# Feed-forward of a hybrid trunk step: borders of the up product rearranged

## The chip, the cores and the metric

The program runs on one core of one Trainium2 chip. The metric is the device time of one execution in microseconds; the median of the runs shown counts. One execution was also taken by the hardware profiler, and all rows below come from it.

## The reference

One layer of a bidirectional hybrid (RWKV-7 and mLSTM) diffusion step on 128 context and 1024 latent tokens, D_MODEL 1024, D_FF 2816, all in float32. The change lies in the last third: the output projection with its norm, and the gated ConvFFN.

```python
x = x + g1 * rmsnorm(merged @ p['w_out'], p['norm_g'][1])
h = rmsnorm(x, p['norm_g'][2]) * (1.0 + sc2) + sh2
u_act, u_val = jnp.split(h @ p['ffn_up'], 2, axis=-1)
u_act = dwconv_grid(u_act, p['ffn_conv'], rows) + p['ffn_conv_b']
f = (jax.nn.silu(u_act) * u_val) @ p['ffn_down']
x = x + g2 * rmsnorm(f, p['norm_g'][3])
```

`dwconv_grid` is a 3x3 depthwise convolution on a grid 64 wide (of width 3 on the context). There are 128 + 1024 = 1152 tokens, T in the kernel.

## The kernel before, in words

Every float32 product is made of reduced-precision parts: an operand is split into a high part (written by ACT, `AF.Copy`) and a low part (DVE, the difference), and TensorE (PE) makes three products of parts. So each weight tile and each activation needs one ACT and one DVE instruction before PE can use it. A scheduler orders the instructions of each engine; where an engine's `.on` is true, its instructions stay in the order in which the code is written. PE is pinned in this way around here, the others are not.

**The output projection** (tile `pwo`, L1500) goes by blocks of 128 tokens, nine of them (NB). Per block: a Square with row sums on ACT (L1516), the gate rows on DVE (`ob`, L1517), the residual (`xt`, L1521), a second Square (L1524), the second norm (`ob`, L1526), and `modulate`: eight transposes on PE (`ptx`), scale and shift on DVE and ACT into `hf` (L1482, L1485), and a store of `hf` to `h2d` in HBM by the DMA queue of SP. The last block's `modulate` is written inside the up product, ahead of unit 4. The gate rows of the second gate are stored (`grd`) at the end of this stage.

**The up product** computes two halves of 22 blocks of 128 columns (`uraw` the convolved half, `uval` the other) by a scheme of seven products P1 to P7 instead of eight. A unit is one product of one block for one half of the tokens (c 0 or 1): 12 matmuls 128x288 into `pu`. The operands of P1, P2 and P3 are quarters X11, X21, X22 of h, those of the others sums of them (T1 to T4), made and split by `x_split` and `x_rest` (L1455, L1456, sums at L1464). Half c=0 is loaded into `x0` and `x1` during the output projection; half c=1 is loaded into the `xb` tiles by `x_mid` and `x_late`, which are written ahead of units 4 and 8. Units 0 to 3 are P1 and P2 of blocks 0 and 1 for c=0, units 4 to 7 the same for c=1, unit 8 is the first P6. The weights come as `wraw`; P6 needs a sum `s` of two quarters, made by POOL (L1625) into the one buffer with tag `hf`, and differences (L1626 on POOL, L1627, L1628 on DVE). `w_split` writes `hl`, high on ACT (L1632), low on DVE (L1633). Products leave `pu` on DVE (L1671 to L1682), P1 on ACT (L1669).

**The convolution** of a finished block (`conv_of`): one bias and scale on ACT (L1637), eight taps and two context operations on DVE (L47, L50), Silu on ACT (L1641), the product with `uval` on POOL (L1642), and a store to `f2d` (L1643). It runs beside the units of the next block. For the blocks in LATE it is put off: `uraw` and `uval` are stored to `latd`, and the convolution is made during the down product by `late_convs`, with tiles `lraw`, `lval` (two buffers) and `lua` (one).

**The down product** has three sweeps over the tokens, of 4, 3 and 2 blocks of 128. The first reads each of the 22 blocks of f once, in the order KO, in which the LATE blocks are the last. `f_group` fetches f in groups of six blocks, by pairs, into `fg` (each pair: a DMA, a split on ACT L1708 and DVE L1709); the buffers of groups 0, 1 and 2 are those of `x1`, `x0` and `x2`. The products go into `pfd`; the weights are split at L1718 and L1719.

```python
PROD = ("P1", "P2", "P6", "P7", "P4", "P5", "P3")
LATE = (1, 5, 9, 13, 17, 21)
KO = [i for i in range(NFB) if i not in LATE] + list(LATE)
s1s[i] = wt.tile([128, 4, 128], F32, name="s1", tag="hf", bufs=1)
if (m, c) == ("P3", 1):
    conving = (put_off if i in LATE else conv)(i)
```

Of the kernel before, what the change touches and what calls it, by code (L numbers as in the profile page):

```python
# [58 lines left out]
def _body(tc, ctx, A, O, dbg, stop):  # L59
# [88 lines left out]
    latd = dram("latd", [6, 2, 128, T])  # L148
# [1238 lines left out]
    with tc.tile_pool(name="br", bufs=1) as bp, tc.tile_pool(name="brl", bufs=2) as bl:  # L1387
# [11 lines left out]
        banks(pg=5, ps=3)  # L1399
# [66 lines left out]

    def modulate(xh, b):

        c = 0 if b == 0 else 1
        for q in range(2):  # L1470
            pt = (pss if b < NB - 1 else psg)([128, 4, 128], "ptx")
            for j in range(4):
                f = 4 * q + j
                pe.transpose(pt[:, j, :], xh[:, 128 * f:128 * f + 128], ident)
            if q == 0 or b == NB - 1:
                hf = wt.tile([128, 4, 128], F32, name="hf", tag="hf", bufs=1)
            else:
                hf = wp.tile([128, 8, 128], F32, name="hf", tag="whi", bufs=2)[:, 0:4]
            for j in range(4):
                f = 4 * q + j  # L1480
                if j % 2:
                    s.activation(hf[:, j, :], pt[:, j, :], AF.Identity, scale=sc2[:, f, c:c + 1],  # L1482
                                 bias=sh2[:, f, c:c + 1])
                else:
                    v.tensor_scalar(hf[:, j, :], pt[:, j, :], sc2[:, f, c:c + 1], sh2[:, f, c:c + 1],  # L1485
                                    op0=ALU.mult, op1=ALU.add)
            dma(h2d[q][:, :, 128 * b:128 * b + 128], hf)

    with tc.tile_pool(name="wo", bufs=1) as wop:
# [15 lines left out]
        for blocks in ((0, 1),) + tuple((b,) for b in range(2, NB)):  # L1505
            pts = {b: [psg([128, 512], "pwo") for q in range(2)] for b in blocks}
            wo_mm(pts, blocks)
            for b in blocks:
                c = 0 if b == 0 else 1
# [35 lines left out]
        rows_out(1, make_scale("g2", 40, 3, 0.0))  # L1545
# [24 lines left out]
    def x_mid():  # L1570

        x_load(1, 0, 0, q11)
        x_load(1, 1, 0, q21)
        x_split(1, "X11", q11, xb[1], xb[2])
        x_split(1, "X21", q21, xb[3], xb[8])
        x_rest(0, ta, tb, (r11, r12, r21, r22), [quarter(x2, i) for i in range(4)])

    def x_late():
        x_load(1, 0, 1, q12)
        x_load(1, 1, 1, q22)  # L1580
        x_split(1, "X22", q22, xb[9], xb[10])
        ta = x_sub(v, x_tmp(), q12, q11)
        tb = x_sub(v, x_tmp(), q22, ta)
        x_rest(1, ta, tb, (q11, q12, q21, q22), [xb[0]] + xb[11:14])

    PROD = ("P1", "P2", "P6", "P7", "P4", "P5", "P3")
# [7 lines left out]
    LATE = (1, 5, 9, 13, 17, 21)  # L1594
# [25 lines left out]
    def w_split(i, m):  # L1620

        a11, a12, a21, a22 = raws[i]
        if m == "P6":
            s1s[i] = wt.tile([128, 4, 128], F32, name="s1", tag="hf", bufs=1)
# [21 lines left out]
    with tc.tile_pool(name="cv", bufs=2) as cv:  # L1646
# [51 lines left out]
        def f_group(sw, j):  # L1698
# [6 lines left out]
            for o in range(0, n, 2):  # L1705
                hi, lo = (t_[:, x, o:o + 2, 0:128 * nb] for x in range(2))
                dma(f32(lo), f2d[6 * j + o:6 * j + o + 2, :, ts].rearrange("k p t -> p k t"))
                s.activation(hi, f32(lo), AF.Copy)  # L1708
                v.tensor_tensor(lo, f32(lo), f32(hi), op=ALU.subtract)  # L1709
                yield  # L1710
# [11 lines left out]
        pe.on = True  # L1722
        conving, ns, wds = None, 0, {}
        w_load()
        w_load()
        for u, (i, m, c) in enumerate(units):
            if u == 4:
                modulate(ob, NB - 1)
                x_mid()
# [7 lines left out]
            if u == 8:  # L1737
                x_late()
            unit(i, m, c)
            if conving:  # L1740
                next(conving, None)
            if (m, c) == ("P3", 1):
# [4 lines left out]
            if i == NFB - 1 and c == 1 and m == "P6":  # L1747
                g0 = f_group(0, 0)
                next(g0)
            if i == NFB - 1 and c == 1 and m == "P4":  # L1750
                wds[0] = wd_split(0)
        for _ in conving:
# [6 lines left out]
    with tc.tile_pool(name="fd", bufs=1) as fd, tc.tile_pool(name="fo", bufs=2) as fo:  # L1759
        gr = rows_in(1, [fd.tile([128, D], F32, name=f"grow{c}") for c in range(2)])  # L1760
# [41 lines left out]
        for sw, (b0, nb) in enumerate(SWEEPS):  # L1802
# [3 lines left out]
            for k in range(no):  # L1806
# [6 lines left out]
                if k == no - 1:  # L1813
# [7 lines left out]
                for _ in range(3 + k % 2):  # L1821
                    next(late, None)
            for _ in late:
# [48 lines left out]
```

## Time and profile before

| | us |
|---|---|
| median of 3 runs | 2272.18 (2268.37 to 2274.38) |
| the profiled execution | 2274.78 |
| its span | 2272.9 |
| PE busy | 2059.0 (91%) |
| DVE busy | 1500.1 (66%) |
| ACT busy | 875.3 (39%) |
| POOL busy | 677.5 (30%) |

Engines: PE is TensorE, DVE VectorE, ACT ScalarE, POOL GpSimd; SP issues most DMAs. Times in a trace are microseconds from the span's start. The rows of windows have the stretch, its length, then busy time (and instructions) of PE, PE's weight loads, DVE, ACT and POOL, the mean granted clock of PE as a share of full speed, the busy share of the DMA engines and GB/s. The rows of a timeline have start, duration, engine, line, operation, names (out<-in), shape, how many instructions stand together, and in brackets the engine's idle time just before and what ended it. The rows of the chain have start, duration and the work that the end of the program goes back to. The rows of waits have what waited for what: us in total, times, the longest.

### The profile page before, as it was taken

The numbers are of one execution on the slowest core, as the hardware profiler recorded it, in microseconds if no ns is written. First come the engines' busy times: TensorE is split into PE (matmuls) and PEld (weight loads), VectorE is DVE, ScalarE is ACT, GpSimd is POOL, SyncE is SP. The second block draws the span as 40 slices with busy tenths as digits, with TensorE's granted clock in tenths as the row PEclk, the third lists the DMA queues.
The fourth block names the chain that finished last, engine by engine and source line by source line (L and its number), as shares of the span: only waits on it lengthen the run. The fifth ranks groups of instructions, "written<-read, shape, count | busy, mean of one in ns | idle before, by whom it ended". The sixth has DMA issues, their size and how long they took to land.

```text
span 2272.9 us, 41306 instructions
## 1 busy us (share of the span) xinstructions
PE 2059.0 (91%) x16579; PEld 1883.0 (83%) x16579; DVE 1500.1 (66%) x2355; ACT 875.3 (39%) x1662; POOL 677.5 (30%) x784
## 2 busy tenths in 40 slices
PE   6999998988889989889989999699999999895998
PEld 4998998978878878878878877699999999674776
DVE  3766778779555556654733445799999999785432
ACT  3664646462233433346421244332223232342322
POOL 2000198888522224355312101122222221111000
PEclk8999999999989999989989999899999999997999
DMA  9144444535745655377666654322121221763543
GB/s 263 53 99 120 121 120 112 146 100 135 190 112 130 157 128 140 109 216 228 193 217 202 223 189 150 89 78 100 57 98 60 97 92 51 289 245 118 199 139 102
DMA packets 405615, 322.06 MB, mean 142 GB/s; under 512 B 92817, under 2 KB 366901, under 8 KB 405424
## 3 DMA queue, kind: packets, MB, share of 16 engines
q1 hardware_dynamic: 302848, 225.78, 33.4%
q10 hardware_dynamic: 89280, 56.32, 8.7%
q0 software_dynamic: 13296, 37.33, 5.3%
q8 instruction: 131, 2.15, 0.4%
q14 instruction: 60, 0.49, 0.1%
HBM read 229.33 MB, written 90.02 MB: 141 GB/s over the span
## 4 chain that ended last, share of the span: by engine, by line
PE 49%; DMA 15%; POOL 12%; DVE 12%; issue 5%; ACT 5%; SPq 1%; ACTq 0%; POOLq 0%; DVEq 0%
PE pu L70 18%; PE pg L399 6%; POOL Lb L546 5%; POOL tmp L544 5%; PE pfd L70 5%; PE pwo L1500 4%; PE pbr L70 4%; PE pg L70 3%; DMA wraw<-in_ffn_down 2%; DVE lua L47 2%; DMA aw<-in_ada_w 1%; DMA La<-Ad 1%; PE pY L70 1%; DVE ua L47 1%; DMA bon<-bond 1%
## 5 line engine op out<-in xcount | busy, mean ns | idle before, releaser
L399 PE MATMUL pg<-act,whi 128*128 128x384 f32 (+1 forms) x1696 | 328.5, 341 | 0.5 <-DVE act L362 0.4
L70 PE MATMUL pu<-x,hl 128*128 128x288 f32 x2024 | 296.1, 297 | 11.3 <-ACT hl L1632 9.3
L399 PEld LDWEIGHTS pg<-act,whi 128*128 128x128 f32 (+1 forms) x1696 | 296.4, 189 | 7.4 <-DVE act L362 0.8
L70 PEld LDWEIGHTS pu<-x,hl 128*128 128x128 f32 x2024 | 280.3, 191 | 12.0 <-ACT hl L1632 9.5
L70 PE MATMUL pu<-xb,hl 128*128 128x288 f32 x1672 | 247.3, 295 | 2.2 <-DVE xb L1456 1.4
L70 PEld LDWEIGHTS pu<-xb,hl 128*128 128x128 f32 x1672 | 230.6, 189 | 3.0 <-DVE xb L1456 1.9
L70 PE MATMUL pfd<-whi,fg 128*128 128x512 f32 x540 | 171.4, 399 | 14.7 <-ACT whi L1718 7.1
L399 PE MATMUL pg<-act,wlo 128*128 128x384 f32 (+1 forms) x848 | 168.7, 338 | 7.8 <-DVE wlo L386 7.8
L47 DVE SCALAR_TENSOR_TENSOR ua<-uraw,par,ua 128x945 f32<-128x945 f32 (+2 forms) x128 | 161.7, 1263 | 11.0 <-ACT ua L1637 11.0
L1632 ACT ACTIVATE hl<-wraw 128x512 fp32r<-128x512 f32 x132 | 81.1, 628 | 207.2 <-PE pu L70 158.4
L399 PEld LDWEIGHTS pg<-act,wlo 128*128 128x128 f32 (+1 forms) x848 | 147.8, 186 | 11.3 <-DVE wlo L386 8.1
L386 DVE TENSOR_TENSOR wlo<-wraw,whi 128x1024 fp32r<-128x1024 f32 (+1 forms) x64 | 80.9, 1267 | 96.4 <-ACT whi L385 96.3
L70 PEld LDWEIGHTS pfd<-whi,fg 128*128 128x128 f32 x540 | 103.0, 192 | 39.4 <-ACT whi L1718 10.1
L546 POOL TENSOR_TENSOR Lb<-Lb,tmp 96x31 f32<-96x31 f32 (+15 forms) x155 | 128.5, 829 | 12.1
L544 POOL TENSOR_TENSOR tmp<-La,Lb 96x31 f32<-96x31 f32 (+15 forms) x155 | 122.6, 791 | 29.1 <-DMA La<-Ad 17.3
L1633 DVE TENSOR_TENSOR hl<-wraw,hl 128x512 fp32r<-128x512 f32 x132 | 124.4, 943 | 2.0 <-ACT hl L1632 2.0
L70 PE MATMUL pfd<-wlo,fg 128*128 128x512 f32 x270 | 108.7, 403 | 8.4 <-DVE wlo L1719 8.1
L70 PE MATMUL pfd<-wr,fg 128*128 128x512 f32 x378 | 88.6, 395 | 26.9 <-ACT fg L1708 24.2
L1642 POOL TENSOR_TENSOR uval<-uval,ua 128x1152 f32<-128x1152 f32 x16 | 44.5, 2782 | 214.9 <-ACT ua L1641 214.9
L70 PEld LDWEIGHTS pfd<-wr,fg 128*128 128x128 f32 x378 | 71.7, 190 | 43.4 <-ACT fg L1708 24.6
L70 PE MATMUL pg<-act,whi 128*128 128x384 f32 x496 | 102.5, 357 | 0.0
L1500 PE MATMUL pwo<-whi,act 128*128 128x512 f32 x288 | 95.7, 410 | 4.0 <-ACT whi L385 4.0
(440 smaller groups left out, 4118.8 us busy)
## 6 DMA issues: line engine op xcount, KB each, us to landing
wraw<-in_ffn_down SPq DMA_DIRECT2D x52, 512.0 KB
wraw<-in_w_in ACTq DMA_DIRECT2D x44, 512.0 KB
wraw<-in_ffn_up SPq DMA_DIRECT2D x44, 512.0 KB
KRd<-KR SPq DMA_DIRECT2D x24, 384.0 KB
sgz<-zraw ACTq DMA_DIRECT2D x16, 576.0 KB
KA<-KRd SPq DMA_DIRECT2D x72, 128.0 KB
BKs<-BKd SPq DMA_DIRECT2D x36, 256.0 KB
suv<-Vd POOLq DMA_DIRECT2D x72, 128.0 KB, 4.1
```

What stands on the lines that cost most here:

```text
L47: v.scalar_tensor_tensor(o, img[:, r0 + i:r1 + i, c0 + j:c1 + j], wt, o, op0=ALU.mult, op1=ALU.add)
L70: return (lambda *a, **k: tc.keep_in_program_order(f(*a, **k))) if self.on else f
L386: v.tensor_tensor(lo, raw, hi.bitcast(F32), op=ALU.subtract)
L399: pe.matmul(out, wt(hw, k), at(ha, k), start=(i == 0), stop=(i == last))
L544: e.tensor_tensor(t3, L[:, j, i].unsqueeze(2).to_broadcast([NI, n, m]), X[:, j:j + 1, c].to_broadcast([NI, n, m]), op=ALU.mult)
L546: e.tensor_tensor(X[:, i, c], X[:, i, c], t3, op=ALU.subtract)
L1500: pe.matmul(pts[b][q], AS[g][:, ha, k, 128 * o:128 * o + 128], wo2[k][hw][:, 0, 512 * q:512 * q + 512], start=(k == 0 and i == 0), stop=(k ...
L1632: s.activation(w[:, 0], src, AF.Copy)
L1633: v.tensor_tensor(w[:, 1], src, f32(w[:, 0]), op=ALU.subtract)
L1642: gp.tensor_tensor(val, val, ua, op=ALU.mult)
```

## The change

- The product order becomes P1, P2, P6, P7, P3, P4, P5; a block's convolution follows P5.
- LATE is (2, 7, 12, 17, 21) in place of (1, 5, 9, 13, 17, 21): five convolutions are put off.
- The sum `s` of block 0 gets its own buffer (one half of a `uval` tile), and the second `hf` of the last block's `modulate` the other half.
- ACT is pinned for the last block of the output projection, and again for the last `modulate` with the splits of X11 and X21 for c=1 behind it. The loads of these quarters, and the operands T1 to T4 for c=0, are written ahead of `x_mid`.
- The first group of f is fetched as two single blocks and two pairs, from P3 of the last block on (P6 before), with a second step at its P4.
- The gate rows are written at unit 60 in the code, and read back in the first down sweep behind k = 9.
- The counts of PSUM banks `pg` and `ps` stand the other way round in one call; the late convolutions advance by 3, 3, 4 steps per k in place of 3, 4.

```diff
-        banks(pg=5, ps=3)
+        banks(ps=3, pg=5)
...
-            if q == 0 or b == NB - 1:
+            if q == 1 and b == NB - 1:
+                hf = spare[0][:, 512:1024].rearrange("p (k n) -> p k n", n=128)
+            elif q == 0:
...
             for b in blocks:
+                s.on = b == NB - 1
...
-        rows_out(1, make_scale("g2", 40, 3, 0.0))
+        s.on = False
...
     def x_mid():
 
-        x_load(1, 0, 0, q11)
-        x_load(1, 1, 0, q21)
+        s.on = True
+        modulate(ob, NB - 1)
         x_split(1, "X11", q11, xb[1], xb[2])
         x_split(1, "X21", q21, xb[3], xb[8])
-        x_rest(0, ta, tb, (r11, r12, r21, r22), [quarter(x2, i) for i in range(4)])
+        s.on = False
+
+    x_load(1, 0, 0, q11)
+    x_load(1, 1, 0, q21)
+    x_rest(0, ta, tb, (r11, r12, r21, r22), [quarter(x2, i) for i in range(4)])
...
-    PROD = ("P1", "P2", "P6", "P7", "P4", "P5", "P3")
+    PROD = ("P1", "P2", "P6", "P7", "P3", "P4", "P5")
...
-    LATE = (1, 5, 9, 13, 17, 21)
+    LATE = (2, 7, 12, 17, 21)
...
-            s1s[i] = wt.tile([128, 4, 128], F32, name="s1", tag="hf", bufs=1)
+            if i == 0:
+                s1s[i] = spare[0][:, 0:512].rearrange("p (k n) -> p k n", n=128)
+            else:
+                s1s[i] = wt.tile([128, 4, 128], F32, name="s1", tag="hf", bufs=1)
...
-            for o in range(0, n, 2):
-                hi, lo = (t_[:, x, o:o + 2, 0:128 * nb] for x in range(2))
-                dma(f32(lo), f2d[6 * j + o:6 * j + o + 2, :, ts].rearrange("k p t -> p k t"))
+            for o, e in ((0, 1), (1, 2), (2, 4), (4, 6)) if sw == j == 0 else ((o, o + 2) for o in range(0, n, 2)):
+                hi, lo = (t_[:, x, o:e, 0:128 * nb] for x in range(2))
+                dma(f32(lo), f2d[6 * j + o:6 * j + e, :, ts].rearrange("k p t -> p k t"))
...
+        spare.append(cvt("uval"))
...
             if u == 4:
-                modulate(ob, NB - 1)
                 x_mid()
...
+            if u == 60:
+                rows_out(1, make_scale("g2", 40, 3, 0.0))
...
-            if (m, c) == ("P3", 1):
+            if (m, c) == (PROD[-1], 1):
...
-            if i == NFB - 1 and c == 1 and m == "P6":
+            if i == NFB - 1 and c == 1 and m == "P3":
                 g0 = f_group(0, 0)
                 next(g0)
             if i == NFB - 1 and c == 1 and m == "P4":
                 wds[0] = wd_split(0)
+                next(g0)
...
-        gr = rows_in(1, [fd.tile([128, D], F32, name=f"grow{c}") for c in range(2)])
+        gr = [fd.tile([128, D], F32, name=f"grow{c}") for c in range(2)]
...
-                if k == no - 1:
+                if k == min(no - 1, 17):
                     next(g3)
...
-                for _ in range(3 + k % 2):
+                for _ in range(3 + (k % 3 == 2)):
                     next(late, None)
+                if sw == 0 and k == 9:
+                    rows_in(1, gr)
```

ACT at the end of the output projection, before (`ob,s2o<-xt` is the last block's second Square, `xb` the splits of the second token half, `hf` the last modulate):

```order
L1669 ACTIVATE uraw<-pu 128x288
L1455 ACTIVATE x_14544<-xs 128x1152
L1455 ACTIVATE xb_14545<-xb_14548 128x1152
L1524 ACTIVATE ob,s2o<-xt_14513 128x1024
L1669 ACTIVATE uraw<-pu 128x288
L322 ACTIVATE s2o<-s2o,eps_130 128x1
L1455 ACTIVATE xb_14547<-xb_14550 128x1152
L1482 ACTIVATE hf<-ptx,modT,sc_13527 128x128
```

and now (the half of `uval` is the second `hf`; instructions of a pinned engine carry the line of the helper, L70):

```order
L1681 ACTIVATE uraw<-pu 128x288
L70 ACTIVATE ob,s2o<-xt_14513 128x1024
L70 ACTIVATE s2o<-s2o,eps_130 128x1
L1455 ACTIVATE x_14540<-xs 128x1152
L1681 ACTIVATE uraw<-pu 128x288
L1644 ACTIVATE hl<-wraw 128x512 x2
L1455 ACTIVATE x_14540<-xs 128x1152
L70 ACTIVATE hf<-ptx,modT,sc_13527 128x128 x2
L70 ACTIVATE uval<-ptx,modT,sc_13527 128x128 x2
L70 ACTIVATE xb_14541<-xb_14544 128x1152
L70 ACTIVATE xb_14543<-xb_14546 128x1152
```

The Square moved ahead of both xb splits, and the xb splits moved behind the four writes of modulate.

SP at the same place, before (`grd` is the store of the gate rows, `h2d` that of hf, `xb` the loads of the second token half):

```order
L76 DMA wraw<-in_ffn_up 128x8x128
L76 DMA h2d<-hf 512x1x128 x2
L76 DMA grd<-g_14531 128x8x1 x2
L76 DMA xb_14548<-h2d 128x4x288
L76 DMA xb_14550<-h2d 128x4x288
L76 DMA x1d<-xt_14513 128x1024
L76 DMA h2d<-hf 512x1x128
L76 DMA xb_14549<-h2d 128x4x288
```

and now:

```order
L76 DMA wraw<-in_ffn_up 128x8x128
L76 DMA h2d<-hf 512x1x128 x2
L76 DMA grd<-g_15666 128x8x1 x2
L76 DMA xb_14544<-h2d 128x4x288
L76 DMA xb_14546<-h2d 128x4x288
L76 DMA x1d<-xt_14513 128x1024
L76 DMA h2d<-hf 512x1x128
L76 DMA h2d<-uval 512x1x128
```

The store of the gate rows stands where it stood before, between the hf stores and the xb loads; the second half of the last hf store now comes out of `uval` and stands ahead of the next xb load.

SP at the end of the up product, before (`fg` are the fetches of f, `latd` the stores of the last block put off, `grow` the loads of the gate rows):

```order
L76 DMA wraw<-in_ffn_down 128x1024 x2
L76 DMA fg<-f2d 128x2x512
L76 DMA latd<-uval 128x1152
L76 DMA fg<-f2d 128x2x512
L76 DMA latd<-uraw 128x1152
L76 DMA fg<-f2d 128x2x512 x2
L76 DMA grow_19967<-grd 128x1024
```

and now:

```order
L76 DMA wraw<-in_ffn_down 128x1024
L76 DMA fg<-f2d 128x512 x2
L76 DMA wraw<-in_ffn_down 128x1024
L76 DMA fg<-f2d 128x2x512 x4
L76 DMA latd<-uval 128x1152
L76 DMA latd<-uraw 128x1152
L76 DMA wraw<-in_ffn_down 128x1024
L76 DMA fg<-f2d 128x2x512
L76 DMA lraw<-latd 128x1152
```

The first fetches are single blocks, the stores of the last block stand behind four pairs, and the gate rows' loads have gone from here to a place behind the first late loads.

## Rows read from the trace of the kernel before

**Rows 1.** Windows: the two borders and the sweep between them.
```profile
1430.00:1470.00 40.00, 26.52 (x161) 25.59 (x162) 29.91 (x41) 15.78 (x25) 7.19 (x4) 0.80 0.25 71
1470.00:1880.00 410.00, 410.00 (x3098) 410.00 (x3098) 381.46 (x565) 122.13 (x194) 106.61 (x64) 1.00 0.25 83
1940.00:2090.00 150.00, 118.03 (x494) 93.70 (x495) 105.90 (x105) 55.23 (x57) 21.39 (x12) 0.91 0.58 215
```

**Rows 2.** Waits of PE, 1290 to 1470.
```profile
PE pu L70 <- ACT hl L1632: 9.3, 1, 9.3
PE ptx L70 <- DVE ob L1526: 6.7, 1, 6.7
...
PE pu L70 <- DVE ob L1517: 2.0, 1, 2.0
```

**Rows 3.** Timeline of PE, 1414 to 1492.
```profile
1417.10 8.16 PE L70 MATMUL pu<-x,hl 128*128 128x288 f32 x48 [2.01 <-DVE ob L1517]
1431.95 1.97 PE L70 MATMUL ptx<-ident,ob 128*128 128x128 f32 x8 [6.69 <-DVE ob L1526]
1433.57 7.33 PE L70 MATMUL pu<-xb,hl 128*128 128x288 f32 x48
1450.17 12.30 PE L70 MATMUL pu<-x,hl 128*128 128x288 f32 x72 [9.28 <-ACT hl L1632]
...
1489.09 1.72 PE L70 MATMUL pu<-x,hl 128*128 128x288 f32 x12
```

**Rows 4.** The chain that ended last, 1400 to 1475.
```profile
1417.11 10.87 DMA xb<-h2d
...
1442.48 3.06 DMA h2d<-hf
...
1445.71 1.69 POOL s L1625
...
1447.47 1.26 POOL wraw L1626
```

**Rows 5.** Timeline of ACT, 1418 to 1450.
```profile
1428.00 1.16 ACT L1455 ACTIVATE xb<-xb 128x1152 fp32r<-128x1152 f32 x1 [4.16 <-DMA xb<-h2d]
1429.07 1.04 ACT L1524 ACTIVATE ob<-xt 128x1024 f32<-128x1024 f32 x1
```

**Rows 6.** Timeline of PE, 1925 to 2085.
```profile
1930.97 1.75 PE L70 MATMUL pu<-xb,hl 128*128 128x288 f32 x12
1939.80 0.79 PE L70 MATMUL pfd<-whi,fg 128*128 128x512 f32 x1 [7.08 <-ACT fg L1708]
...
2079.87 0.79 PE L70 MATMUL pfd<-wr,fg 128*128 128x512 f32 x1 [24.20 <-ACT fg L1708]
```

**Rows 7.** The chain that ended last, 1925 to 2090.
```profile
1933.59 5.08 DMA fg<-f2d
```

**Rows 8.** Timeline of POOL, 1940 to 2090 (first and last of six).
```profile
1968.88 2.65 POOL L1642 TENSOR_TENSOR lval<-lval,lua 128x1152 f32<-128x1152 f32 x1 [33.84 <-ACT lua L1641]
...
2069.06 2.60 POOL L1642 TENSOR_TENSOR lval<-lval,lua 128x1152 f32<-128x1152 f32 x1 [15.43 <-ACT lua L1641]
```

**Rows 9.** Timeline of POOL, 1730 to 1860 (products of the convolutions).
```profile
1757.06 2.81 POOL L1642 TENSOR_TENSOR uval<-uval,ua 128x1152 f32<-128x1152 f32 x1 [14.07 <-ACT ua L1641]
...
1796.57 2.78 POOL L1642 TENSOR_TENSOR uval<-uval,ua 128x1152 f32<-128x1152 f32 x1 [14.07 <-ACT ua L1641]
...
1821.14 2.79 POOL L1642 TENSOR_TENSOR uval<-uval,ua 128x1152 f32<-128x1152 f32 x1 [14.07 <-ACT ua L1641]
```

**Rows 10.** Timeline of DVE, 1796 to 1850 (low parts of hl).
```profile
1797.08 2.81 DVE L1633 TENSOR_TENSOR hl<-wraw,hl 128x512 fp32r<-128x512 f32 x1
...
1821.65 2.82 DVE L1633 TENSOR_TENSOR hl<-wraw,hl 128x512 fp32r<-128x512 f32 x1
...
1846.24 2.84 DVE L1633 TENSOR_TENSOR hl<-wraw,hl 128x512 fp32r<-128x512 f32 x1
...
1849.37 0.68 DVE L1633 TENSOR_TENSOR hl<-wraw,hl 128x512 fp32r<-128x512 f32 x1
```

**Rows 11.** Timeline of DVE, 1410 to 1480 (the last block's residual).
```profile
1422.56 1.28 DVE L1521 SCALAR_TENSOR_TENSOR xt<-ob,rso,xt 128x1024 f32<-128x1024 f32 x1
```

More of the change, by code (lines that the diff above doesn't have):

```diff
@@ L147, in _body @@
     f2d = dram("f2d", [NFB, 128, T])
-    latd = dram("latd", [6, 2, 128, T])
+    latd = dram("latd", [5, 2, 128, T])
     wp = pool("wp", 2)
@@ L1465, in x_sub @@
         return out
+    spare = []
     def modulate(xh, b):
@@ L1580, in x_late @@
         x_load(1, 1, 1, q22)
-        x_split(1, "X22", q22, xb[9], xb[10])
         ta = x_sub(v, x_tmp(), q12, q11)
         tb = x_sub(v, x_tmp(), q22, ta)
+        x_split(1, "X22", q22, xb[9], xb[10])
         x_rest(1, ta, tb, (q11, q12, q21, q22), [xb[0]] + xb[11:14])
-    PROD = ("P1", "P2", "P6", "P7", "P4", "P5", "P3")
+    PROD = ("P1", "P2", "P6", "P7", "P3", "P4", "P5")
     XOP = dict(P1="X11", P2="X21", P6="T2", P7="T3", P4="T4", P5="T1", P3="X22")
```

## The prediction

> **What bounds the kernel now.** I read the windows by stage first. From 1470 to 1880 us PE is busy for all of its 410 us at a granted clock of 1.00, with DVE at 381.46 beside it: the up product of the feed-forward is PE's, and DVE has 28.5 us to spare. On both sides PE is not full: 26.52 of 40 us at a clock of 0.80 from 1430 to 1470, and 118.03 of 150 at 0.91 from 1940 to 2090 [rows 1]. So only those two borders can give time back, and only the stage between them can lose it. The waits of PE say what ends the idle time at the first border: 9.3 us for a weight tile's high part on ACT, 6.7 for the last normalised block, 2.0 for the eviction before it [rows 2]. PE's timeline places them: 48 matmuls from 1417.10, the eight transposes at 1431.95 after 6.69 idle, 48 more from 1433.57, product P6 at 1450.17 after 9.28 idle; the third block's units begin at 1489.09 [rows 3]. The chain shows why P6 is late: the store of hf goes out at 1442.48 and takes 3.06, and only then does POOL write the sum s at 1445.71 (1.69), since s lives in hf's only buffer, then a difference of 1.26, and then the split [rows 4]. ACT shows why the transposes are late: the split of xb at 1428.00 stands ahead of the last block's Square, because its load, issued at 1417.11, took 10.87 [rows 4, 5]. At the second border the units end at 1930.97 + 1.75 = 1932.7; the first fetch of f leaves at 1933.59 and lands 5.08 later, and PE starts at 1939.80 after 7.08 idle [rows 6, 7]. Much later it waits 24.20 us, until 2079.87, for the last pair of f, the longest wait behind the sweep [rows 6]. The six convolutions put off feed that pair: their products on POOL begin at 1968.88 and end with the one at 2069.06 [rows 8].
>
> **What sets the pace in the sweep.** One unit of 12 matmuls is a fourteenth of a block. Twenty blocks run from 1489.09 to 1932.7, so a block is 22.18 us and a unit 1.585. In neighbouring blocks that have a convolution, the products on POOL follow each other by 24.57 us (1796.57 to 1821.14) [rows 9]: DVE needs 2.4 us more than PE for such a block. Across a put-off block they are 39.51 apart (1757.06 to 1796.57), against 44.36 for two blocks on PE, so DVE caught up the 4.8 of a run of three there. The reserve can be read too. In the first, second and third block of a run, the long split of hl ends at 1799.89, 1824.47 and 1849.08 [rows 10]; PE comes to P6 of the block, four units behind its start, at 1805.9, 1828.1 and 1850.3 (counted back from 1932.7 by 22.18). The slack is 6.0, 3.6 and 1.2 us. No wait of PE stands in this stretch, and a fourth block would lack 1.2.
>
> **The change, part by part.** The time is summed against the profiled execution: 2274.78 us, of which 2272.9 is span. It is 2.6 above the median of 2272.18, so 2.6 comes off at the end.
>
> *Gate rows written later.* In SP's order the store stays where it was, behind the last hf store and ahead of the xb loads. Nothing moves at this border: 0 us. The loads of the gate rows move behind the first late loads; they are needed only at the end of the first down sweep, 0 us.
>
> *Bank counts exchanged.* The first unit still follows the same DVE eviction, so the 2.01 us gap stays: 0.
>
> *Own buffer for the first sum, and ACT's order.* POOL can now add right behind the last eviction (1417.1) instead of at 1445.71. The 9.28 us wait as such disappears. Square no longer stands behind the xb split: its input xt is written from 1422.56 to 1423.84 as before [rows 11], and from Square's start to the transposes there were 2.9 us (1429.07 to 1431.95) [rows 3, 5], so the transposes start at about 1427.5, some tenths for the queue included, instead of 1431.95. But the splits of xb now stand behind the four hf writes of modulate on ACT. Modulate ends there at about 1431.5, then come two splits of 1.16 [rows 5] and their low parts on DVE, about as long, so the second 48 matmuls start at 1436 to 1437.7 where they started at 1433.57. PE waits there for xb instead, about 7.5 us. The 48 take 6.3 to 7.3 [rows 3], so P6 starts at 1443 to 1447; I take 1445.5, 4.7 earlier. From P6 to the third block lie 20 units: 31.7 us at 1.585, and they took 38.9 (1450.17 to 1489.09). The 7.2 between are units at the lower of PE's two clock levels after the wait, 1.2 instead of 2.4 GHz (72 matmuls in 12.30 instead of 9.5), and short gaps behind operands. About half of this should go, 3.8, since a wait of similar length now comes four units earlier. **Border 1: -8.5**, with ends -12 (all 7.2 gone) and -1 (P6 3.7 later, by the next lines).
>
> POOL's sum now meets a busy DVE. The row shows what that costs: the split of hl that starts 0.5 us behind a POOL product takes 2.82 instead of 0.68 and ends 0.54 us behind the product [rows 9, 10]. POOL's two operations, 1.69 + 1.26 = 2.95, could hold up DVE at 1417 to 1421 for that long, ahead of xt. I take nothing, as xt was no earlier before (two operations of x, as long as a split, stood ahead of it), and keep -1 as the end. The Trainium skill, in "SBUF — State Buffer", section "Who interferes with whom", says that a DVE operation with two SBUF inputs and a GpSimd operation that reads SBUF exclude each other for a whole instruction. That speaks against the early sum: by it the order of issue would decide, and the time would be up to 3 us longer, about 2249. The long hl rows agree with it.
>
> *Third product earlier, first fetch by single blocks.* P3 is the last reader of the buffer that the first group of f goes into. It now ends five units, 7.9 us, ahead of the sweep's end, and the first fetch is half as large. DVE still has the low part of the third fetch ahead of the last evictions; PE waits for these, 2 to 4 us instead of 7.08 + 0.47. Worth 4 to 5, but only up to the wait for the last pair, which takes it back. It counts there.
>
> *Five convolutions put off instead of six.* The blocks are now 2, 7, 12, 17 and 21: runs of two, four, four, four and three with a convolution. The sweep gets one more on DVE, and three runs have a fourth block. Each lacks 1.2 us by the slacks above; I take 1.4, a little more, since these readings are good to some tenths. **Sweep: +4.2.** Ends: 0 if a reserve appears that the rows do not show, +15 if a put-off block no longer catches up what four have built up, 9.6 us. Of this it gave 4.8 in the rows, with DVE idle for part of the 28.5 us that the window has left.
>
> *The chain of the late convolutions.* The first product on POOL was 36.2 us behind the sweep's end, and six of them span 100.2 us, a step of 20.0 [rows 8]; from the last to PE 10.8 (2069.06 to 2079.87). Five make 36.2 + 80.2 + 10.8 = 127.2 behind the end; the loads come up to 3 us earlier now that fetching begins inside the sweep, so 124.1 to 127.2, and I take 125.6 where it was 147.2. **Late chain: -21.6.** PE reaches that pair some 4 us earlier (its start) than the 123 us of before (2055.7), so it still waits 6 to 10. If the chain fell below 118, PE would be the bound: -28.8 is the end of this term; with the sweep's step of 24.57 for two of the five it would be -12.5.
>
> **Sum.** -8.5 + 4.2 - 21.6 = -25.9. Span 2247.0, profiled time 2248.9, median about **2246 us**.
>
> **Rivals.** *The late chain stops being the bound.* Five convolutions are done before PE needs them, and the wait for f goes altogether: -28.8 in place of -21.6, with border 1 at -10, makes 2238. For it: DVE idles between late convolutions. Against it: their steps do not change in kind. 13%.
>
> *The border is not mended, and DVE lags more.* Border 1 gives only 3, as the xb loads (10.87) and ACT's order take over, and the fourth blocks cost 4 us each: -3 + 12 - 21.6 is -12.6, so 2259.6. For it: the gate rows' store still stands ahead of the loads. 22%.
>
> *DVE sets the pace of the whole sweep.* Four blocks with a convolution and one without need 4 x 24.57 = 98.3 us plus the put-off block; PE's five take 110.9. What is left for the put-off block is 12.6. Across one, DVE took 39.51 - 24.57 = 14.9 with its waits in it. Should its work really be above 12.6, the lag never clears and each of the 17 blocks costs 2.4: +40.5 - 8.5 - 21.6 makes +10.4, **2282.6**, slower. Against it: 28.5 us of idle DVE in the window, of which these 14.9 must hold some. 3%.
>
> *It does not do what it says.* Two parts already don't (gate rows, banks). If the late chain also keeps its length, because another store or load in SP's queue sets it, there remain 4 to 8 us: 2264 to 2268. 5%.
>
> **Numbers.** 0.3% of 2272 is 6.8 us, about what a measurement can tell from no change. Forecast 57%, the rivals 13, 22, 3 and 5. Faster by over 0.3% (below 2265.4) are the first three and half of the last: 0.93. Within: 0.04. Slower: 0.03. The range takes in the first rival's 2238 and the second's 2259.6 with the open ends of the border (3 us) and of the runs: 2233 to 2263.
>
> **What would show it.** PE's waits: no 9.3 for hl at P6; a wait for ob of some 2; a new one for xb of about 7; a first wait for fg of 2 to 4, a last one of 6 to 10. In the sweep three short waits for hl, at the fourth blocks 6, 11 and 16. POOL's late products: five, 20 apart. I am wrong where waits in the sweep come in every block, the last wait for fg stays above 15, or P6 starts later than 1450.

## The result, and the profile after

The changed kernel takes 2242.23 us (median of 4, 2239.66 to 2243.86) beside 2273.28 (median of 4, 2268.37 to 2276.34): a ratio of 0.9864, interval 0.9844 to 0.9885, so 31 us or 1.4% faster. The forecast was 2246, range 2233 to 2263. The profiled execution has a span of 2242.0, against 2272.9.

The windows of the changed kernel, over the same stretches of the clock as [rows 1] (its stages stand some 6 to 28 us earlier in them):

```profile
1430.00:1470.00 40.00, 35.47 (x249) 35.13 (x250) 35.89 (x52) 18.48 (x26) 7.59 (x4) 0.88 0.34 96
1470.00:1880.00 410.00, 407.57 (x3074) 405.70 (x3073) 390.80 (x569) 122.07 (x194) 123.91 (x66) 1.00 0.24 79
1940.00:2090.00 150.00, 137.34 (x574) 109.35 (x573) 107.99 (x114) 58.20 (x70) 18.69 (x10) 0.97 0.64 223
```

PE gains 9 us of work at the first border and 19 at the second, and loses 2.4 in the sweep, where it was full before. PE's waits in the changed kernel, 1290 to 1470 us:

```profile
PE pu L70 <- ACT xb L70: 12.2, 1, 12.2
...
PE pu L70 <- DVE ob L1522: 2.0, 1, 2.0
PE ptx L70 <- DVE ob L1531: 1.2, 1, 1.2
```

from 1470 to 1925:

```profile
PE pu L70 <- DVE hl L1645: 1.8, 4, 0.8
PE pu L70 <- DVE uval L1689: 0.7, 4, 0.2
```

and from 1900 to the end (its longest ones):

```profile
PE pfd L70 <- ACT whi L1730: 7.5, 5, 2.6
PE pfd L70 <- DVE uraw L1692: 6.1, 1, 6.1
...
PE pfd L70 <- ACT fg L1720: 5.1, 1, 5.1
```

The 9.3 for P6 and the 6.7 for the transposes of [rows 2] have become one wait of 12.2 for xb; the sweep has small waits that it did not have; the 24.20 of [rows 6] is 5.1. PE's timeline gives the places, which answer to [rows 3] and [rows 6]:

```profile
1411.53 8.41 PE L70 MATMUL pu<-x,hl 128*128 128x288 f32 x48 [2.00 <-DVE ob L1522]
1421.14 1.09 PE L70 MATMUL ptx<-ident,ob 128*128 128x128 f32 x8 [1.20 <-DVE ob L1531]
1434.46 9.18 PE L70 MATMUL pu<-xb,hl 128*128 128x288 f32 x48 [12.23 <-ACT xb L70]
1443.48 9.75 PE L70 MATMUL pu<-x,hl 128*128 128x288 f32 x72
...
1929.61 1.19 PE L70 MATMUL pfd<-whi,fg 128*128 128x512 f32 x2 [6.11 <-DVE uraw L1692]
...
2053.14 17.71 PE L70 MATMUL pfd<-wr,fg 128*128 128x512 f32 x68 [0.47 <-DVE fg L1721]
```

The transposes follow the norm at once, but the second 48 matmuls stand 12 us behind them. ACT's timeline in the changed kernel says why:

```profile
1425.83 1.15 ACT L1644 ACTIVATE hl<-wraw 128x512 fp32r<-128x512 f32 x2 [5.74 <-DMA x1d<-xt]
...
1430.14 0.46 ACT L70 ACTIVATE hf<-ptx,modT,sc 128x128 f32<-128x128 f32 x1 [2.11 <-DVE hf L1489]
...
1433.26 2.20 ACT L70 ACTIVATE xb<-xb 128x1152 fp32r<-128x1152 f32 x2
```

A split of hl, which the scheduler put ahead of modulate, waits until the store of xt to `x1d` has left the buffer that it is to be written to; modulate and the xb splits queue behind it on ACT, and modulate's part on DVE behind the low part of an x split that follows it. The chain that ended last has the store, with its start and duration:

```profile
1417.25 8.48 DMA x1d<-xt
```

Two things speak from outside the stages that the prediction looked at. In the kernel before, the first product of the branch stage, a thousand us into the program, had stood idle (PE's timeline):

```profile
1153.59 2.90 PE L70 MATMUL pbr<-y2r,whi 128*128 128x384 f32 x8 [6.54 <-issue]
```

and in the changed kernel it has not:

```profile
1148.22 1.55 PE L70 MATMUL pbr<-y2r,whi 128*128 128x384 f32 x8
```

That is the stage for which the exchanged bank counts are set. And the last 190 us, whose code is unchanged, took 191.8 us from the last pair of f to the end before and 188.9 now; over all profiled runs below they took 188.9 to 196.3.

So single runs scatter by several us, and I read each part from its stretch of the trace, in us. "First unit" is the start of the first up unit, "P6" that of the first P6, "end" the sweep's, "pair" the matmuls behind the last pair's low part (2081.13 before, 2053.14 now). In e7, e8 and e12 the down product follows without a gap, and its start is the end; in e8 PE has no wait at the pair, and its place is counted by matmuls.

| run | first unit at | to P6 | to the sweep's end | to the last pair | to the end | span |
|---|---|---|---|---|---|---|
| before | 1417.1 | 33.1 | 482.5 | 148.4 | 191.8 | 2272.9 |
| changed | 1411.5 | 32.0 | 480.0 | 129.6 | 188.9 | 2242.0 |
| e1 banks | 1415.1 | 32.9 | 482.6 | 147.9 | 192.8 | 2271.3 |
| e2 five late | 1413.1 | 32.7 | 488.1 | 131.5 | 193.2 | 2258.6 |
| e3 first border | 1413.2 | 31.3 | 476.4 | 149.1 | 194.4 | 2264.4 |
| e4 second border | 1419.1 | 32.8 | 479.9 | 147.3 | 196.3 | 2275.4 |
| e5 hl behind | 1412.0 | 27.6 | 479.9 | 129.3 | 193.7 | 2242.5 |
| e6 three buffers | 1422.4 | 32.7 | 480.5 | 124.1 | 189.3 | 2249.0 |
| e7 ring kept | 1415.5 | 32.8 | 480.2 | 128.4 | 194.5 | 2251.3 |
| e8 three edits | 1408.2 | 28.1 | 479.1 | 123.5 | 190.4 | 2229.3 |
| e9 gate rows later | 1415.6 | 28.4 | 479.9 | 128.7 | 192.1 | 2244.7 |
| e10 banks back | 1410.5 | 33.0 | 480.3 | 128.7 | 193.1 | 2245.5 |
| e11 changed again | 1412.5 | 32.9 | 480.3 | 127.7 | 190.9 | 2244.3 |
| e12 three edits again | 1405.4 | 28.2 | 479.2 | 124.1 | 189.6 | 2226.4 |

### The profile page after: what moved, and what is told of

Read it like the earlier page. It is cut to its first block, busy times and chain, and to the rows that moved or that the text cites. A ratio compares the mean times of both kernels' runs of the same rounds, so it can differ in the third digit from the quotient of the medians.

```text
span 2242.0 us, 41274 instructions
## 1 busy us (share of the span) xinstructions
PE 2053.5 (92%) x16579; PEld 1878.5 (84%) x16579; DVE 1508.6 (67%) x2356; ACT 873.5 (39%) x1663; POOL 694.0 (31%) x784
## 4 chain that ended last, share of the span: by engine, by line
PE 40%; DVE 20%; DMA 13%; POOL 12%; issue 8%; ACT 5%; SPq 1%; ACTq 0%; DVEq 0%; POOLq 0%
PE pfd L70 7%; PE pg L399 6%; DVE ua L47 6%; PE pu L70 5%; POOL Lb L546 5%; POOL tmp L544 5%; PE pwo L1504 4%; PE pg L70 4%; PE pbr L70 4%; DMA wraw<-in_ffn_down 2%; DVE hl L1645 2%; DMA aw<-in_ada_w 2%; DMA La<-Ad 1%; PE pY L70 1%; PE pmN L70 1%
## 5 line engine op out<-in xcount | busy, mean ns | idle before, releaser
L70 PE MATMUL pu<-x,hl 128*128 128x288 f32 x2024 | 294.5, 296 | 3.8 <-DVE ob L1522 2.0
L70 PEld LDWEIGHTS pu<-x,hl 128*128 128x128 f32 x2024 | 277.5, 189 | 5.3 <-DVE hl L1645 2.9
L70 PE MATMUL pu<-xb,hl 128*128 128x288 f32 x1672 | 247.6, 296 | 13.0 <-ACT xb L70 12.2
L70 PEld LDWEIGHTS pu<-xb,hl 128*128 128x128 f32 x1672 | 230.7, 189 | 14.5 <-ACT xb L70 12.5
L47 DVE SCALAR_TENSOR_TENSOR ua<-uraw,par,ua 128x945 f32<-128x945 f32 (+2 forms) x136 | 177.3, 1304 | 12.4 <-ACT ua L1649 12.4
L70 PE MATMUL pfd<-whi,fg 128*128 128x512 f32 x540 | 172.8, 402 | 13.6 <-ACT whi L1730 7.5
L70 PEld LDWEIGHTS pfd<-whi,fg 128*128 128x128 f32 x540 | 104.2, 194 | 37.7 <-ACT whi L1730 9.9
L1645 DVE TENSOR_TENSOR hl<-wraw,hl 128x512 fp32r<-128x512 f32 x132 | 134.1, 1025 | 0.0
L546 POOL TENSOR_TENSOR Lb<-Lb,tmp 96x31 f32<-96x31 f32 (+15 forms) x155 | 128.8, 831 | 12.2
L70 PE MATMUL pfd<-wlo,fg 128*128 128x512 f32 x270 | 109.2, 404 | 5.4 <-DVE wlo L1731 5.3
L1637 POOL TENSOR_TENSOR s<-wraw 128x512 f32<-128x512 f32 x21 | 41.9, 1994 | 212.3 <-DVE hl L1645 193.0
L70 PE MATMUL pg<-act,whi 128*128 128x384 f32 x496 | 103.2, 359 | 0.0
L1731 DVE TENSOR_TENSOR wlo<-wraw,whi 128x1024 fp32r<-128x1024 f32 x45 | 58.5, 1299 | 64.8 <-ACT whi L1730 64.6
L385 ACT ACTIVATE whi<-wraw 128x1024 fp32r<-128x1024 f32 (+1 forms) x64 | 66.7, 1047 | 81.3 <-PE pg L399 35.0
```

The lines of the kernel that those rows point to most:

```text
L47: v.scalar_tensor_tensor(o, img[:, r0 + i:r1 + i, c0 + j:c1 + j], wt, o, op0=ALU.mult, op1=ALU.add)
L70: return (lambda *a, **k: tc.keep_in_program_order(f(*a, **k))) if self.on else f
L385: s.activation(hi, raw, AF.Copy)
L546: e.tensor_tensor(X[:, i, c], X[:, i, c], t3, op=ALU.subtract)
L1637: gp.tensor_tensor(s1s[i], a21, a22, op=ALU.add)
L1645: v.tensor_tensor(w[:, 1], src, f32(w[:, 0]), op=ALU.subtract)
```

## The experiments

The theory: five convolutions in place of six give most of it (some 19 us less in the late chain, some 4 more in the sweep), the first border gives 8, and the banks, in another stage, some 5. The rivals: DVE pays back more of it in the sweep, the borders only move their waits, the banks do nothing.

**One part at a time on the kernel before** (before 2269.25, median of 31).

```diff
-        banks(pg=5, ps=3)
+        banks(ps=3, pg=5)
```

> The kernel before with the two PSUM bank counts exchanged in the one call, nothing else. Theory: the first branch product no longer takes a bank that the stage before still evicts, so the 6.5 us of idle PE ahead of it goes, and the first unit of the up product, at 1417.1 before, starts some 5 us earlier; nothing behind it gives that back: about -5 us. Rival, the prediction's step: the exchange does nothing, the 6.5 us stay, 0 us.

2267.56, ratio 0.9979 (0.9965 to 0.9994): -1.4 to -7.9 us. So it is faster; the theory's 5 lies inside, and the two medians differ by 1.7. The first branch product starts without a wait, at 1148.26, but the first up unit stands only 2 us earlier than in the profile of before.

```diff
-    LATE = (1, 5, 9, 13, 17, 21)
+    LATE = (2, 7, 12, 17, 21)
...
-                if k == no - 1:
+                if k == min(no - 1, 17):
...
-                for _ in range(3 + k % 2):
+                for _ in range(3 + (k % 3 == 2)):
```

> The kernel before with five convolutions put off instead of six (blocks 2, 7, 12, 17, 21, with the order of f that follows and the 3, 3, 4 steps), nothing else. Theory: one step of 20 us less in the late chain, no earlier loads, so the last pair of f comes 20 us earlier behind the sweep's end, its wait falls from 24.2 to about 4; the sweep pays some 3 us in waits at the fourth blocks: -17 us. Rival: DVE lags in the whole sweep, which pays 12 or more: -8 us or less gain, and PE waits for hl in many blocks.

2259.65, ratio 0.9945 (0.9925 to 0.9966): -8 to -17 us. From the sweep's end to the last pair it takes 16.9 less (131.5 against 148.4); the sweep pays 5.6 (488.1 against 482.5). PE's waits in its sweep, 1490 to 1925:

```profile
PE pu L70 <- DVE uraw L1680: 5.0, 3, 1.7
```

Three waits, one for each run of four blocks, as foreseen in number, not one in each block: the rival in which DVE sets the pace of the whole sweep has fallen. They are waits for an eviction (`uraw`), not for hl. The last wait for fg was 7.0, not 4. The first product (36.1 behind the end) and the steps (20.1) are as priced; what is longer, by 3.0, is the tail from the last product to the pair: the product takes 3.46 (2.60 before), its store 4.89 (3.11) and the load 4.01 (3.60).

The third kernel has the hunks on `spare`, `s.on`, `x_mid` and the own buffer of `s1`, and one that the diff in front leaves out with its "...": in `x_late` the split of X22 stands behind the two differences. It has nothing else.

> The kernel before with the parts at the first border alone: own buffer for the first sum and for the second hf, ACT pinned, the loads and operands written earlier. Theory: from the first unit to the end of the sweep some 6 us less: P6 starts only 1 to 2 us earlier, since PE now waits 12 us for xb behind a high part on ACT that waits for the store of x1d, and the rest comes from units at full clock behind P6: -6 us. Prediction's step: -8.5. Rival: the wait has only changed its place, 0 us.

2264.08, ratio 0.9975 (0.9959 to 0.9992): -2 to -9 us. From the first unit to the sweep's end it takes 507.7 instead of 515.6: -7.9, near the prediction's 8.5 and beyond my -6. Only 1.8 of it is P6; 6.1 come behind it.

The fourth has the product order, the first fetches by single blocks (from P3 on) and the step at P4 alone.

> The kernel before with the product order and the first fetches of f alone (third product fifth, two single blocks, a second step at P4). Theory: PE starts the down product 1 to 4 us earlier, and waits that much longer for the last pair of f, because six late convolutions still set its time; only the up to 3 us by which they begin earlier remain: 0 to -3 us. Rival: what the border gives stays, -4 to -5 us.

2265.41, ratio 0.9974 (0.9956 to 0.9993): -2 to -10 us. The trace splits this: from the sweep's end to the last pair 147.3 instead of 148.4, so the border itself gave 1.1 at most, as the theory had it (its wait for the last pair is still 23.8; e1 and e3, which leave this stretch alone, have 147.9 and 149.1). But the stretch from P6 to the end is 2.6 shorter, which neither side expected: P3 ahead of P4 and P5 lets the first two blocks run with one wait for xb of 1.4 in place of 2.2 in three; that is a part of it, the rest stays open.

By their ratios the four parts give 4.8, 12.5, 5.7 and 5.9 us, 29 together, beside the 31 of the whole change. With intervals 6 to 10 us wide this fits, and does not show that nothing else counts.

**Edits on the changed kernel** (timed later, beside the kernel before again: 2272.89, median of 11).

```diff
         x_split(1, "X21", q21, xb[3], xb[8])
-        s.on = False
...
                 if j < NFB and all((j - 2, p_) in HLs for p_ in PROD):
                     w_load()
+            s.on = False
```

> The changed kernel with ACT kept pinned over the weight splits written at unit 4, so that they stand behind the splits of xb. Theory: the 12.2 us of PE before unit 4 contain 5.7 us in which ACT stood at a split of hl whose buffer the store of x1d still held, with modulate queued behind it; these go, unit 4 starts 4 to 5 us earlier after the first unit and P6 as much: -4 us against the changed kernel. Rival: the xb loads themselves are late, or DVE is, and the wait stays above 10: 0 to -1.

2241.82, ratio to before 0.9875 (0.9847 to 0.9903); against the changed kernel's 0.9864 no gain can be seen in that. The trace shows the step: unit 4 waits 7.4, and P6 comes 27.6 behind the first unit instead of 32.0.

```profile
1430.60 9.14 PE L70 MATMUL pu<-xb,hl 128*128 128x288 f32 x48 [7.40 <-ACT xb L70]
1439.58 9.52 PE L70 MATMUL pu<-x,hl 128*128 128x288 f32 x72
```

The 4.4 us pass through the sweep whole (479.9 against 480.0); in this profile the last 190 us took 4.8 longer.

```diff
-                raw, val = (fo.tile([128, T], F32, name=nm, tag=nm) for nm in ("lraw", "lval"))
+                raw = fo.tile([128, T], F32, name="lraw", tag="lr", bufs=3)
+                val = fo.tile([128, T], F32, name="lval", tag="lval")
...
-                yield from conv_of(i, raw, val, fd.tile([128, T], F32, name="lua", tag="lua"))
+                yield from conv_of(i, raw, val, fo.tile([128, T], F32, name="lua", tag="lr", bufs=3))
```

> The changed kernel with three buffers shared by lraw and lua in the late convolutions, so that the next one can begin while Silu and the product of the last still use theirs. Theory: a step of the late chain loses the 4 us in which DVE waits for the bias on ACT, the chain falls below PE's own path, the last wait for fg (5.1 us) goes: -5 us, and no more than that. Rival: the step is set by DVE's other work and the loads, 0 to -1.

2242.82, ratio to before 0.9867 (0.9834 to 0.9900). PE has no wait for ACT at the last pair any more, and reaches it 124.1 behind the sweep's end instead of 129.6. DVE's waits in the down product, 1930 to 2060, show the cause; without the edit, in the changed kernel, and with it:

```profile
DVE lua L47 <- ACT lua L1649: 8.9, 4, 4.2
```

```profile
DVE lua L47 <- ACT lua L1649: 4.4, 4, 1.6
```

The medians don't show the 5 us here either. Nor does this profile's span: its first unit started 11 us late, ahead of anything that the edit touches.

```diff
     fst.close()
-    banks(pg=8)
     with tc.tile_pool(name="fd", bufs=1) as fd, tc.tile_pool(name="fo", bufs=2) as fo:
```

> The changed kernel without the new PSUM pools ahead of the down product: its first tile takes the next bank of the running ring instead of the one evicted last. Theory: the 6.1 us of PE at the second border fall to 1 or 2, but the last wait for fg grows from 5.1 to 9 or 10, since the late chain sets that time: 0 us. Rival: the border counts by itself, -4 to -5 us.

2253.54, ratio to before 0.9914 (0.9883 to 0.9945). At the border PE now waits 1.9 us instead of 6.1, and the last pair still comes 128.4 behind the sweep's end. That lies inside the 127.7 to 129.6 of the kernels without this edit and e6's (changed, e5, e9, e10, e11), so all of the 4.2 us is taken back, as the theory said. Its way was another: the last wait did not grow (4.7); up to the pair PE waits 5.9 for low parts of weights where it waited 2.6. Why the timed runs are slower than those of the changed kernel is not settled; the stretches of the trace differ by 4 at the first unit and 5.6 in the unchanged tail.

> The changed kernel with the three edits together (splits of hl behind xb, three buffers for the late convolutions, the PSUM ring kept). Theory: the first border gives 4, the last wait goes (5), and with it the second border counts at last (4): -13 us against the changed kernel, some 2229. Rival: the late chain, shorter by less than 9, still ends behind PE, and the second border is taken back: -9 at most.

The three edits together: 2238.62, ratio to before 0.9857 (0.9826 to 0.9887), with one profile of 2229.3. The times don't tell one expectation from the other, since the changed kernel was not timed beside it. The trace does for one point: PE starts the down product without a gap (a wait of 1.9 follows its first matmul), has no wait at the last pair, and still reaches it only 123.5 behind the sweep's end. In e6, with the border's wait of 6.1, it was 124.1. Up to the pair PE waits 7.2 for low parts of weights here, and 2.8 in e6. So the second border does not count here either.

**Beside the changed kernel as measure** (before 2270.33, median of 11).

> The changed kernel as it is, once more, beside the next three on one chip, as their measure: 2242 within some 5 us, and the same waits (12 us for xb at unit 4, 6 at the second border, 5 for the last pair of f).

2248.32 (2243.49 to 2255.26), ratio to before 0.9900 (0.9873 to 0.9927): 6 us above the first measurement, just beyond the 5 expected. The three waits are there again, with 13.6, 6.1 and 4.0.

> The kernel with the three edits once more. Theory, from its trace: from the first unit of the up product to the end it took 821.1 us where the changed kernel took 830.5, so -9 us against the changed kernel on the same chip. Rival, from its timed runs (2238.6 against 2242.2, other chips): -3 to -4, because what the borders give is lost in the two last down sweeps, whose waits for weights grow.

2230.94 (2228.23 to 2235.78), ratio to before 0.9826 (0.9799 to 0.9852): 17 us below the changed kernel beside it, more than the theory's 9. By the table, the two profiles differ by 4.7 up to P6, 1.1 up to the sweep's end, 3.6 up to the last pair and 1.3 behind it; the other 7.1 lie ahead of the first unit, which none of the edits touches, and are there already at the first branch product (1135.89 against 1143.35). This version beats the kernel before in both of its measurements, and the changed kernel where they stand side by side; how much more than the 9.4 of the stretches it is worth (3.6 against the changed kernel's first measurement, 17 here) stays open. In its timeline the down product starts without a gap at 1912.69, and the last pair has no wait for ACT:

```profile
1912.69 0.40 PE L70 MATMUL pfd<-whi,fg 128*128 128x512 f32 x1
1914.98 0.69 PE L70 MATMUL pfd<-whi,fg 128*128 128x512 f32 x1 [1.89 <-DVE fg L1720]
...
2036.79 15.71 PE L70 MATMUL pfd<-wr,fg 128*128 128x512 f32 x68 [0.73 <-DVE fg L1720]
```

```diff
-        banks(ps=3, pg=5)
+        banks(pg=5, ps=3)
```

> The changed kernel with the two bank counts as they were before. Theory: the idle 6 us ahead of the first branch product come back, +5 us against the changed kernel on the same chip. Prediction's step: 0 us.

2251.02, ratio to before 0.9908 (0.9884 to 0.9932): 2.7 above the changed kernel, with intervals that overlap. The wait is back:

```profile
1151.92 2.90 PE L70 MATMUL pbr<-y2r,whi 128*128 128x384 f32 x8 [8.18 <-issue]
```

but its first up unit stands at 1410.5, no later than 1412.5.

```diff
                 rows_out(1, make_scale("g2", 40, 3, 0.0))
+                v.on = False
+            if u == 59:
+                v.on = True
             unit(i, m, c)
```

> The changed kernel with DVE pinned from unit 59 on until the gate row is made, so that its store really comes later, behind the loads of xb and the store of x1d. Theory: the store of x1d, 8.5 us in the changed kernel, lands 2 to 4 us earlier, so ACT's split of hl, modulate and unit 4 come as much earlier, and the 12.2 us wait falls to 8 to 10: -2 to -4 us. Rival: the store is small (4 KB) and costs the others nothing: 0 us.

2244.27, ratio to before 0.9881 (0.9853 to 0.9910): 4.0 below the changed kernel, intervals overlapping. The trace is clear. P6 comes 28.4 behind the first unit instead of 32.9, and ACT's split of hl no longer waits for the store; PE and then ACT in this kernel:

```profile
1434.49 9.72 PE L70 MATMUL pu<-xb,hl 128*128 128x288 f32 x48 [8.16 <-ACT xb L70]
```

```profile
1425.26 0.63 ACT L1644 ACTIVATE hl<-wraw 128x512 fp32r<-128x512 f32 x1 [1.08 <-DVE ob L1531]
```

The store of x1d went out at 1421.35 here, so it was done in less than 3.9 us. What changed is the company: the DMA view of the changed kernel, 1405 to 1430, with the gate rows' store, and then that of this one, 1409 to 1434, without:

```profile
DMA packets 5378, 2.79 MB, mean 111 GB/s; under 512 B 2176, under 2 KB 5248, under 8 KB 5376
...
q1 hardware_dynamic: 5376, 2.76, 52.0%
```

```profile
DMA packets 3825, 3.04 MB, mean 122 GB/s; under 512 B 111, under 2 KB 3695, under 8 KB 3823
...
q1 hardware_dynamic: 3823, 3.02, 37.3%
```

The row of the queue has packets, MB, and the time of the packets as a share of the 16 DMA engines' time: fewer bytes took a larger share with the small stores than without. The loads of xb and the store of x1d go out at the same distance from the first unit in both kernels (0.0 and 5.7), so what differs there is the small stores. Two stores of 4 KB make some 2060 small packets, and with them the store of x1d lands after 8.48 us instead of less than 3.9. The Trainium skill, in "DMA: Bandwidth & Descriptors", section "Specifications", gives 512 B as the least transfer for the full rate; the two rows agree, as far as they can show it.

## Why the prediction was right

It was right in time (2246 against 2242.2) and in its two largest terms; the rest came to the right sum by errors that cancel.

- **The late chain** was forecast at -21.6 and gave -18.8 (2053.14 less 1923.50 against 2081.13 less 1932.72). The first product came 33.2 behind the sweep's end, inside the 33.2 to 36.2. Two terms were mis-sized: the steps were 20.6 on the mean, not 20.0, which is 2.3 over four of them, and the tail was 12.7 (2039.17 to 2051.88), not 10.8, taken from [rows 8] and [rows 6]. Its pieces stand in the chains, before and then now; a weight load issued at 2041.18 stands beside the store now, and none does before:

```profile
2069.06 2.60 POOL lval L1642
2071.96 3.11 DMA f2d<-lval
2075.13 3.60 DMA fg<-f2d
```

```profile
2039.17 2.86 POOL lval L1654
2042.32 4.63 DMA f2d<-lval
2047.02 3.73 DMA fg<-f2d
```

e2, with this part alone, has -16.9, so some 2 of the 18.8 are the rest of the change; the first product came 36.1 behind the end there. The last wait of PE was 5.1, just below the 6 to 10 foreseen, and that is luck: the pair came 2.8 later than forecast, and PE came to it 4.3 later than forecast (123.3 behind the sweep's end, not 119).
- **The sweep** was forecast at +4.2 with three short waits for hl at the fourth blocks. They came at P6 behind the fourth convolution's product, as priced, but the places were named wrongly: that product falls two blocks behind its block, so the waits stand in blocks 8, 13 and 18 (1617.74, 1729.57, 1841.47), not 6, 11 and 16, 0.3 each, with one of 0.8 in block 3 (1505.83), where the first border's delay was still being worked off, and 0.7 in all for an eviction behind each. Block 8 has the pattern:

```profile
1616.19 1.22 PE L70 MATMUL pu<-x,hl 128*128 128x288 f32 x8
1617.74 0.79 PE L70 MATMUL pu<-x,hl 128*128 128x288 f32 x4 [0.34 <-DVE hl L1645]
1618.71 1.85 PE L70 MATMUL pu<-xb,hl 128*128 128x288 f32 x12 [0.17 <-DVE uval L1689]
1620.40 1.72 PE L70 MATMUL pu<-x,hl 128*128 128x288 f32 x12
```

The two units take 4.2 us there (4.7 in block 3) where two units take 3.2. By the 336 matmuls of the first two blocks, the third block starts at 1475.3 now and at 1489.1 before [rows 3]; from there to the end it is 448.2 against 443.6, +4.6, which is these four places. The visible waits are 2.5 of that. In e2, without the new product order, it was 5.6.
- **The first border** was forecast at -8.5 by P6 4.7 earlier and 3.8 behind it. It gave -8.2 (from the first unit to the third block, 63.8 against 72.0), but by 1.1 and 7.1; e3 alone gives -7.9 up to the sweep's end. The step that failed is "the second 48 matmuls start at 1436 to 1437.7", with what follows from it. Behind the shifted first unit that would have been 1430 to 1432, and was 1434.46. It priced modulate and the xb splits on ACT, and not the split of hl ahead of them, which the order showed: modulate ended at 1433.36, not at the shifted 1425.9. A second error made up for a good half of that: PE started when the first xb split was written, 1.1 behind modulate, and not 4.5 to 6.2. And the 48 took 9.0, not 6.3 to 7.3, at a granted clock of 0.71 (1434.40 to 1443.40) after the 12.23 of idle time; the first 48 of [rows 3] had taken 8.16 after 2.01. e5 and e9 take ACT's wait away in two ways, with 4.4 and 4.5 us at P6. Behind P6, all of the slow units and gaps went (7.1 of 7.2), not half.
- **The gate rows** were costed at 0, since their store did not move. That is right for this change; e9 shows what moving it is worth, 4.5 us at P6. The rows that showed it stood there: the xb load of 10.87 behind the store [rows 4] was taken as it was, without asking why it took so long.
- **The banks** were the wrong step: "the first unit still follows the same DVE eviction, so the 2.01 us gap stays: 0". The gap did stay (2.00), but the call stands at the head of the branch stage, and the wait that it ended was 5.9 to 8.2 us at that stage's first product, in the five profiles with the old counts. What is left of it in the end is less: e1 has 1.4 to 7.9, e10 2.7 with intervals that overlap. From that product to the first up unit it takes 256.4 to 263.5 us in the five, and 262.9 to 270.7 in the nine with the new counts. One wait of PE behind that product stands in these nine alone, 2.7 to 6.0 for a split of `zraw` on ACT; in the changed kernel:

```profile
PE pmod L70 <- ACT zraw L768: 2.7, 1, 2.7
```

So most of the gain is taken back ahead of the up product: on the mean the nine start the branch stage 8.3 earlier, and the first up unit 1.5 earlier. Little of the 5.6 between the two profiles compared can be put down to this part; the first unit scatters from 1405 to 1422 among runs with the same code ahead of it.
- **The second border** was said to count only up to the wait for the last pair. e4 and e7 agree: what they gain there (1.1, and 4.2 less of wait) leaves no more at the pair than profiles differ by. But the late chain is not the only thing that takes it back, as the prediction had it. PE's own way from the sweep's end to the pair, without its wait there, is 122.2 to 123.9 us in all fourteen profiles, with a wait of 1.9 at the border as with one of 9.2. "PE reaches that pair some 4 us earlier" holds in none of the nine with the whole change (122.4 to 123.9, beside 123.0 before). PE's wait at the border was 6.1 for an eviction, not 2 to 4.
- **POOL's early sum.** DVE's operation beside it took 2.42 instead of 1.36, and POOL's difference 2.29 instead of 1.26, by the changed kernel's timelines of DVE and of POOL:

```profile
1411.73 2.42 DVE L1456 TENSOR_TENSOR x<-xs,x 128x1152 fp32r<-128x1152 f32 x1 [0.19 <-ACT x L1455]
```

```profile
1413.01 2.29 POOL L1638 TENSOR_TENSOR wraw<-wraw 128x512 f32<-128x512 f32 x1
```

DVE then waits 1.1 for POOL's difference, ahead of xt. Even so xt is no later than before: 4.4 us behind the first unit now (1415.94), 5.5 before. By the rule of the Trainium skill in "SBUF — State Buffer", section "Who interferes with whom", the two exclude each other; the trace agrees, but the time was not 3 us longer for it.

The terms as measured, -5.6 ahead of the first unit, -3.6 from there to the sweep's end, -18.8 to the pair and -2.9 behind it, make -30.9, the whole difference of the spans. The first and the last of these, 8.5 together, are not in the forecast, which by stretches was -25.9 and met -22.4; they lie inside the scatter of the other profiles. The second measurement, 0.9900 or 22.7 us, is near the -22.4. That the first time came within 4 us of the forecast is in part luck.

One sum of the forecast does not come out: its first three chances and half of the last make 0.945, not 0.93.

## What to carry to other kernels

A chain that ends late behind a stage can be worth more than the gap at the stage's head: shorten it first, since it takes back whatever the head gives. And look at what feeds the main engine between the two: here the gain at the head was lost in waits for weights even where the chain had stopped being the bound (e8). Where an engine's order is pinned in part, look at the instructions that a scheduler leaves between the pinned ones, and at who still holds the buffer that each of them writes. A call that sets buffers acts at the head of its own stage; look for its wait there, however far that is from the edits around it.

## What the runs showed of the hardware that was not expected

- Two 4 KB stores of single elements, some 2060 packets under 512 B, delayed what was issued behind them: a 512 KB store took 8.48 us to land (1417.25 to 1425.73), and less than 3.9 without them (e9).
- The exchange of two bank counts took away 6.5 us of idle PE, at the first product of its stage (5.9 to 8.2 over the profiles), of which 1.5 on the mean were left 265 us later. Why is not shown: the profile names no releaser for that wait ("issue"), and no run tells which bank the product gets.
- The same code takes 188.9 to 196.3 us in the last stretch and lets the up product start anywhere between 1405 and 1422; medians of 4 to 6 runs taken at different times could not tell 5 us (the same two kernels differ by 6 and 8 between two such times), while stretches of the trace could (the changed kernel's way from P6 to the sweep's end: 480.0 and 480.3).
